# A hybrid attention block on one core: separate scrap tiles and ScalarE-issued first loads in the output projection, and the plain pair of the down projection moved to the end of its second half

## The chip, the cores and the metric

The kernel runs on one core of a Trainium2 chip. The metric is device time in microseconds of one execution. Before the change three executions took 3287.35, 3281.6 and 3287.61 us (median 3287.35).

## What is computed

One trunk layer on x of 2048 tokens by 1024 channels, in float32. `u` is the normalised input; a combined input projection feeds forgetting attention (8 heads) and an RWKV-7 scan (8 heads), whose outputs stand side by side. What the change touches comes after that:

```python
mix = concatenate([o_fox, o_rwkv], axis=-1) @ w_out      # 2048x1024 @ 1024x1024
h = h + rmsnorm(mix, attn_norm_post)
z = rmsnorm(h, ffn_norm_pre)
f = (silu(z @ w_gate) * (z @ w_up)) @ w_down             # 1024 -> 2816 -> 1024
h = h + rmsnorm(f, ffn_norm_post)
```

## The kernel before

All products run as three fp32r matmuls (`mm3`, lines 76 to 80): each operand is split into a high part (a ScalarE cast) and a low part (a subtraction on VectorE or GpSimd), and high x high, high x low and low x high are summed in PSUM. The kernel is written with a tile framework: a tile pool hands out buffers by tag, an instruction that needs a buffer waits for the last reader of what was in it, and a scheduler orders each engine's instructions by program order and by when it thinks them ready; each engine and each DMA queue then runs strictly in that order. The stages follow each other in time as: input projection, attention with the scan woven in (to about 1611 us), mix, gate and up (from about 1911 us), down (from about 2796 us).

**The mix** (class `Mix`, lines 1010 to 1169). `project` walks the 16 token tiles of 128 in pairs, in the order `m.tiles` (2 to 7, 0, 1, 8 to 15; line 1020). For each pair and each half d of the 1024 output columns it makes one product of 24 matmuls per tile into a PSUM bank of pool `e_q` (6 banks), 32 products in all; ScalarE then squares the bank into a scrap tile `njunk` for the row sums (line 1119) and copies it to `na` (line 1120; 3 buffers). `fetch` (1069) loads a tile's attention output in two halves `er` from DRAM on the SP queue, and `load` (1076) splits them into `emh` and `eml`. The first half of the first tile in this order is fetched at the end of `phase_b` (line 1205), the others in `project`. `others` loads and splits the second half of the output weights.

`norm` (1133) follows a tile: it loads x into `nx` (2 buffers), makes the factor, scales `na` on VectorE (1144), adds x on GpSimd (1145), squares again on ScalarE into `njunk` (1147), stores h, scales (1152, ScalarE), transposes eight blocks on TensorE (1158), scales into `nz` on VectorE (1160) and stores z by the SP queue (1161). The scrap tiles and the z tiles have the same tag:

```python
junk = m.pn.tile([128, 512], BF16, tag="nz", name="njunk")    # lines 1118 and 1146
zs = m.pn.tile([128, 4, 128], F32, tag="nz", name="nz")       # line 1159
```

Pool `e_n` has two buffers for that tag. `weave` (line 1722) interleaves projecting, norms and the start of the FFN (`Ffn.start`: first weights, and from the moment that eight tiles are normed the loads and splits of z for the first half, lines 1297 to 1337). `ffn.open` then makes the FFN's pools in the space that the mix's weights and tiles leave, and `quad` begins its products (`gp`).

**The down projection** (lines 1478 to 1695). The 2048 tokens are two halves of 1024, each of two blocks of 512 tokens (`b`), each of four tiles (`tt`). The 2816 hidden channels are 11 pairs of 256. Ten pairs go in five chunks of two through a seven-product scheme (Winograd's form of Strassen's) over two token blocks and two column blocks: `down_prep` makes the operands `dop` (casts at 1538, subtractions at 1540, differences at 1550), `multiply` forms the products 1, 7, 6, 5, 2, 3, 4 (line 1681), each for four tiles in 6 matmuls a tile, and `put` adds them to accumulators `acc` (the first time a ScalarE copy, line 1642; then VectorE, 1645). The 11th pair is multiplied plainly, four products of four tiles, into the accumulators 2 to 5. In both halves this happens in the first chunk (n == 0, lines 1568 to 1578 and 1685 to 1695). In the last chunk `result` (1657) combines the accumulators (1661 to 1669): a2 and a3 are the columns of token block 0, a4 and a5 those of block 1; `finish` (1613) squares them (ScalarE, 1619), makes the factor (1620, 1621, 69 to 73), multiplies by factor and gain in one instruction (1625) and adds the residual `fht` (1626: GpSimd, and VectorE for the last block of the second half), then stores. The accumulators have one buffer each, so the second half's first write of an accumulator waits for the first half's last reader.

Of the kernel before, what the change touches and what calls it, by code (L numbers as in the profile page):

```python
# [10 lines left out]
F32 = mybir.dt.float32  # L11
# [998 lines left out]
class Mix:  # L1010


    def __init__(m, k, tc, ctx, ins, scr):
        m.k, m.nc, m.ins, m.scr = k, tc.nc, ins, scr
# [54 lines left out]
    def fetch(m, tt):  # L1069
        t = slice(tt * 128, (tt + 1) * 128)  # L1070
        for i in range(2):
            r = m.r([128, 4, 128])
            m.nc.sync.dma_start(out=r, in_=m.scr["mixT"][i * 512:(i + 1) * 512, t].rearrange("(j p) t -> p j t", p=128))
            m.raws[tt, i] = r
# [14 lines left out]
    def project(m, ready):  # L1089
# [3 lines left out]
        ops = {tt: m.load(tt) for tt in m.tiles[0:2]}  # L1093
        others = m.others()
        for p in range(0, n, 2):
# [4 lines left out]
            for d in range(2):  # L1100
                for e, tt in enumerate(pair):
# [16 lines left out]
                    junk = m.pn.tile([128, 512], BF16, tag="nz", name="njunk")  # L1118
# [14 lines left out]
    def norm(m, tt, a, s2):  # L1133
# [8 lines left out]
        for d in range(2):  # L1142
# [3 lines left out]
            junk = m.pn.tile([128, 512], BF16, tag="nz", name="njunk")  # L1146
# [61 lines left out]
class Ffn:  # L1208
# [304 lines left out]
    def down_prep(f):  # L1513
# [41 lines left out]
        for i, (half, n, pairs) in enumerate(seq):  # L1555
# [12 lines left out]
            if n == 0:  # L1568
# [13 lines left out]
            if n > 0 and i + 1 < len(seq):  # L1582
                which = 1 - which
                nxt = load(i + 1)
# [7 lines left out]
            raw = nxt  # L1592

    def down(f):
# [3 lines left out]
        with ExitStack() as ctx:  # L1598
# [14 lines left out]
            def finish(t0, parts, ht, last):  # L1613
                sq = p1.tile([128, 512], F32, tag="fsq", name="fsq")
                s2 = p1.tile([128, 2], F32, tag="fs2", name="fs2", bufs=4)
                ss = p1.tile([128, 1], F32, tag="fss", name="fss", bufs=4)
                rs = p1.tile([128, 1], F32, tag="frs", name="frs", bufs=4)
                for d, a in enumerate(parts):
                    nc.scalar.activation(sq, a, AF.Square, accum_out=s2[:, d:d + 1])
# [3 lines left out]
                for d, a in enumerate(parts):  # L1623
                    c = slice(d * 512, (d + 1) * 512)
                    V.scalar_tensor_tensor(a, a, rs, gp[:, c], op0=ALU.mult, op1=ALU.mult)  # L1625
                    (V if last else G).tensor_tensor(ht[:, c], ht[:, c], a, op=ALU.add)
# [9 lines left out]
            for half in range(f.NHALF):  # L1636
                acc, hts = {}, {}
# [18 lines left out]

                def result(i, tt):
# [9 lines left out]
                    elif i in (3, 4):  # L1667
                        b, parts = (0, (a2, a3)) if i == 3 else (1, (a4, a5))
                        V.tensor_tensor(parts[4 - i], parts[4 - i], a6 if i == 3 else a7, op=ALU.add)  # L1669
                        t0 = half * f.TH + b * f.TQ + tt * 128  # L1670
                        ht = hts.get((tt, b)) or residual(p1.tile([128, D], F32, tag="fht", name="fht", bufs=4), t0)
                        finish(t0, parts, ht, half == f.NHALF - 1 and b == 1)

                for n in range(last + 1):
                    if n == last and half == f.NHALF - 1:
                        for tt in range(NT):
# [80 lines left out]
```

## Time and profile before

| | us |
|---|---|
| median of three executions | 3287.35 |
| the profiled execution, time | 3288.36 |
| its span, first to last instruction | 3286.7 |
| TensorE (PE) busy | 3015.9 |
| VectorE (DVE) busy | 2279.5 |
| ScalarE (ACT) busy | 1573.7 |
| GpSimd (POOL) busy | 1408.8 |

Busy time is summed over the span; matmul ends are modelled, so a full PE is not PE at its peak. Rows of waits name the waiting instruction, then what it waited for. In rows of a timeline a bracket at the end is the time that the engine stood idle ahead of the instruction, and what released it. SPq is the DMA queue that SyncE issues, POOLq that of GpSimd. The granted clock is a share of 2.4 GHz; 0.5 is the lower level of 1.2 GHz.

### The profile page before, as it was taken

How to read it: one execution, taken by the hardware profiler on the slowest of the kernel's cores; microseconds unless marked ns; L12 is line 12 of the kernel's file. 1: busy time of each engine (PE TensorE's matmuls, PEld its weight loads, DVE VectorE, ACT ScalarE, POOL GpSimd, SP SyncE). 2: the span in 40 equal slices, each digit the busy share in tenths (PEclk: the TensorE clock that was granted, in tenths of full speed). 3: DMA queues.
4: the chain of work that ended last, by engine and by line, in shares of the span. 5: the costliest groups of instructions: out<-in, count | busy, mean ns of one | idle time of the engine just before them, and what ended most of it. 6: DMA issues, size and time to landing. Idle time of an engine off the chain costs nothing. (4 is left out here: it accounts for less than half of the span.)

```text
span 3286.7 us, 48864 instructions
## 1 busy us (share of the span) xinstructions
PE 3015.9 (92%) x16913; PEld 2508.6 (76%) x16913; DVE 2279.5 (69%) x4846; ACT 1573.7 (48%) x3325; POOL 1408.8 (43%) x1098
## 2 busy tenths in 40 slices
PE   7999999999899999999797589999999999998895
PEld 5777777777788889888685477788788887786684
DVE  6876687665577777777545455655866556589898
ACT  5444444433677777777543332333433333544442
POOL 3444454444111111111233367433543334788886
PEclk9999999999999999999898789999999999999997
DMA  4756666667434334332345356322322223442552
GB/s 130 193 146 174 188 161 163 161 174 203 145 109 119 103 102 118 102 118 66 99 132 169 115 180 220 113 77 89 104 93 88 90 77 133 165 151 96 188 171 77
DMA packets 466877, 435.67 MB, mean 133 GB/s; under 512 B 137684, under 2 KB 383494, under 8 KB 464582
## 3 DMA queue, kind: packets, MB, share of 16 engines
q1 hardware_dynamic: 440118, 400.48, 39.8%
q0 software_dynamic: 6912, 19.93, 2.0%
q10 hardware_dynamic: 19600, 12.13, 1.4%
q8 instruction: 135, 2.21, 0.3%
q14 instruction: 112, 0.92, 0.1%
HBM read 303.59 MB, written 128.84 MB: 132 GB/s over the span
## 5 line engine op out<-in xcount | busy, mean ns | idle before, releaser
L255 POOL TENSOR_TENSOR wl<-wraw,wh 128x1024 fp32r<-128x1024 f32 (+1 forms) x108 | 268.8, 2492 | 289.7 <-ACT wh L254 287.5
L1266 ACT CAST wh<-fraw 128x512 fp32r<-128x512 f32 x308 | 186.1, 618 | 412.3 <-PE gp L79 205.7
L1270 POOL TENSOR_TENSOR wl<-fraw,wh 128x512 fp32r<-128x512 f32 x132 | 184.5, 1398 | 420.0 <-ACT wh L1266 415.4
L78 PE MATMUL mm<-uh,wh 128*128 128x512 f32 (+1 forms) x864 | 348.4, 404 | 1.1 <-DVE ol L527 1.1
L80 PE MATMUL mm<-uh,wl 128*128 128x512 f32 (+1 forms) x864 | 345.3, 400 | 0.0
L79 PE MATMUL mm<-ul,wh 128*128 128x512 f32 (+1 forms) x864 | 344.8, 399 | 0.0
L78 PE MATMUL gp<-dop 128*128 128x512 f32 x624 | 244.9, 398 | 33.3 <-ACT acc L1642 25.9
L79 PE MATMUL gp<-dop 128*128 128x512 f32 x624 | 245.6, 395 | 1.7 <-POOL dop L1540 1.7
L80 PE MATMUL gp<-dop 128*128 128x512 f32 x624 | 244.1, 395 | 0.0
L976 POOL TENSOR_TENSOR ot<-ot,rb 64x256 f32<-64x256 f32 x64 | 46.3, 723 | 426.1 <-ACT rb L975 426.1
L1540 POOL TENSOR_TENSOR dop<-dcol,dop 128x512 fp32r<-128x512 f32 x140 | 215.2, 1553 | 28.2 <-ACT dop L1538 20.4
L78 PE MATMUL gp<-za,wh 128*128 128x512 f32 x528 | 210.1, 398 | 6.6 <-ACT na L1120 5.0
L1270 DVE TENSOR_TENSOR wl<-fraw,wh 128x512 fp32r<-128x512 f32 x176 | 155.4, 883 | 84.8 <-ACT wh L1266 80.9
L955 DVE TENSOR_TENSOR tl<-pt,th 128x512 fp32r<-128x512 f32 (+1 forms) x280 | 162.8, 592 | 71.3 <-ACT th L953 68.1
L79 PE MATMUL gp<-za,wh 128*128 128x512 f32 x528 | 209.6, 397 | 0.0
L80 PE MATMUL gp<-za,wl 128*128 128x512 f32 x528 | 209.5, 397 | 0.0
L909 DVE CUSTOM_DVE_ANT_0 P<-S,ng 128x512 f32<-128x512 f32 (+2 forms) x320 | 183.8, 605 | 28.3 <-PE pt L947 15.4
L1538 ACT CAST dop<-draw 128x512 fp32r<-128x512 f32 x160 | 97.7, 620 | 220.3 <-PE gp L80 89.1
L78 PEld LDWEIGHTS mm<-uh,wh 128*128 128x128 f32 (+1 forms) x864 | 165.0, 191 | 43.1 <-issue 3.5
L1645 DVE TENSOR_TENSOR acc<-gp,acc 128x512 f32<-128x512 f32 x256 | 167.3, 680 | 42.5 <-PE gp L80 42.2
L80 PEld LDWEIGHTS mm<-uh,wl 128*128 128x128 f32 (+1 forms) x864 | 165.4, 191 | 37.4 <-issue 0.2
L920 ACT ACTIVATE P<-P,nmx 128x896 f32<-128x896 f32 (+7 forms) x248 | 187.5, 761 | 13.3 <-DVE nmx L914 12.7
(382 smaller groups left out, 8568.8 us busy)
## 6 DMA issues: line engine op xcount, KB each, us to landing
wraw<-in_w_in SPq DMA_DIRECT2D x104, 512.0 KB
fraw<-in_ffn_w_gate SPq DMA_DIRECT2D x22, 1024.0 KB
fraw<-in_ffn_w_up SPq DMA_DIRECT2D x22, 1024.0 KB
scr_hid<-s SPq DMA_DIRECT2D x22, 1024.0 KB
draw<-scr_hid SPq DMA_DIRECT2D x22, 1024.0 KB
scr_a<-A SPq DMA_DIRECT2D x16, 1280.0 KB
A<-scr_a SPq DMA_DIRECT2D x64, 320.0 KB
dcol<-scr_wt SPq DMA_DIRECT2D x40, 512.0 KB
```

What stands on the lines that cost most here:

```text
L78: nc.tensor.matmul(out, lhsT=wh, rhs=xh, start=first, stop=False)
L79: nc.tensor.matmul(out, lhsT=wh, rhs=xl, start=False, stop=False)
L80: nc.tensor.matmul(out, lhsT=wl, rhs=xh, start=False, stop=last)
L255: nc.gpsimd.tensor_tensor(wl[:, :, 0:m], raw[:, :, 0:m], wh[:, :, 0:m], op=ALU.subtract)
L909: nc.vector.tensor_tensor_reduce(out=P[:, c0:c0 + n], in0=S[:, 0:n], in1=ng[c0 // 512][:, 0:n], op0=ALU.add, op1=ALU.max, scale=1.0, scala ...
L920: nc.scalar.activation(P[:, x0:x1], P[:, x0:x1], AF.Exp, bias=nmx, accum_out=ls[:, qi, i:i + 1])
L955: nc.vector.tensor_tensor(tl[:, w[0], w[1]], pt[:, w[0], w[1]], th[:, w[0], w[1]], op=ALU.subtract)
L1266: f.nc.scalar.copy(h, x)
L1270: e.tensor_tensor(l[:, c], x[:, c], h[:, c], op=ALU.subtract)
L1538: f.nc.scalar.copy(r[0][p][i], x)
L1540: e.tensor_tensor(r[1][p][i], x, r[0][p][i], op=ALU.subtract)
L1645: V.tensor_tensor(a, ps, a, op=ALU.add)
```

## The change

It has three parts.

1. In the mix the squares' scrap has a tag of its own, `nj` (two buffers of 1 KB a partition).
2. The attention outputs of the first two tiles in the order are loaded by the ScalarE queue, and their loads and splits in `project` are made at high priority of the scheduler.
3. In the second down half the plain pair is no longer multiplied in the first chunk but behind the last one, as four products `direct` into the accumulators that `result` has completed, without the difference that the seven-product form needed; its hidden activations and weights are loaded as a sixth chunk would be, and the residuals go to the slots that the last chunk's loads leave and to `fht`. In both halves the epilogue is written anew: the gain is multiplied in by an instruction of its own (GpSimd for the first column half, VectorE for the second) beside the square, and the last scaling adds the residual in the same VectorE instruction, in place.

```diff
--- before.py
+++ after.py
@@ -1011,7 +1011,7 @@
 
 
     def __init__(m, k, tc, ctx, ins, scr):
-        m.k, m.nc, m.ins, m.scr = k, tc.nc, ins, scr
+        m.k, m.tc, m.nc, m.ins, m.scr = k, tc, tc.nc, ins, scr
         m.pw = [ctx.enter_context(tc.tile_pool(name="e_w", bufs=1, side="right"))]
         m.pr = ctx.enter_context(tc.tile_pool(name="e_r", bufs=1, side="right"))
         m.w = [[None] * NJ, [None] * NJ]
@@ -1070,7 +1070,7 @@
         t = slice(tt * 128, (tt + 1) * 128)
         for i in range(2):
             r = m.r([128, 4, 128])
-            m.nc.sync.dma_start(out=r, in_=m.scr["mixT"][i * 512:(i + 1) * 512, t].rearrange("(j p) t -> p j t", p=128))
+            (m.nc.scalar if tt in m.tiles[0:2] else m.nc.sync).dma_start(out=r, in_=m.scr["mixT"][i * 512:(i + 1) * 512, t].rearrange("(j p) t -> p j t", p=128))
             m.raws[tt, i] = r
 
     def load(m, tt):
@@ -1090,7 +1090,8 @@
 
         nc = m.nc
         n = m.k.T // 128
-        ops = {tt: m.load(tt) for tt in m.tiles[0:2]}
+        with m.tc.high_priority():
+            ops = {tt: m.load(tt) for tt in m.tiles[0:2]}
         others = m.others()
         for p in range(0, n, 2):
             a = {}
@@ -1115,7 +1116,7 @@
                     if d == e and p + 2 + d < n:
                         ops[m.tiles[p + 2 + d]] = m.load(m.tiles[p + 2 + d])
                     c = slice(d * 512, (d + 1) * 512)
-                    junk = m.pn.tile([128, 512], BF16, tag="nz", name="njunk")
+                    junk = m.pn.tile([128, 512], BF16, tag="nj", name="njunk")
                     nc.scalar.activation(junk, ps, AF.Square, accum_out=a[tt][1][:, d:d + 1])
                     nc.scalar.copy(a[tt][0][:, c], ps)
                     if d == 1:
@@ -1143,7 +1144,7 @@
             c = slice(d * 512, (d + 1) * 512)
             nc.vector.scalar_tensor_tensor(a[:, c], a[:, c], rs, m.g[:, c], op0=ALU.mult, op1=ALU.mult)
             nc.gpsimd.tensor_tensor(x[:, c], a[:, c], x[:, c], op=ALU.add)
-            junk = m.pn.tile([128, 512], BF16, tag="nz", name="njunk")
+            junk = m.pn.tile([128, 512], BF16, tag="nj", name="njunk")
             nc.scalar.activation(junk, x[:, c], AF.Square, accum_out=s2[:, d:d + 1])
             yield
         nc.gpsimd.dma_start(out=scr["h"][t, :], in_=x)
@@ -1565,7 +1566,7 @@
             add(s2, a22, s3, ALU.subtract)
             with_column(s2)
             yield
-            if n == 0:
+            if n == 0 and half < f.NHALF - 1:
                 which = 1 - which
                 h, w = f.down_load(f.hslots[which], (hid[half], f.NP - 1), (f.ins["ffn_w_down"][0], f.NP - 1))
                 for t in range(2):
@@ -1579,9 +1580,9 @@
             add(s1, a21, a22, ALU.add)
             with_column(s1)
             yield
-            if n > 0 and i + 1 < len(seq):
+            if nxt is None:
                 which = 1 - which
-                nxt = load(i + 1)
+                nxt = load(i + 1) if i + 1 < len(seq) else f.down_load(f.hslots[which], (hid[half], f.NP - 1), (f.ins["ffn_w_down"][0], f.NP - 1))
             with_column(a12)
             yield
             add(s4, a12, s2, ALU.subtract)
@@ -1590,6 +1591,11 @@
             with_column(a22)
             yield
             raw = nxt
+        h, w = raw
+        f.spare = f.hslots[1 - which]
+        for t in range(2):
+            ops([h[:, j, t] for j in range(2)], [w[:, j, t] for j in range(2)])
+            yield
 
     def down(f):
         nc, tc, scr, out = f.nc, f.tc, f.scr, f.out
@@ -1610,20 +1616,22 @@
                 nc.scalar.dma_start(out=ht, in_=scr["h"][t0:t0 + 128, :])
                 return ht
 
-            def finish(t0, parts, ht, last):
+            def square(a, s2, d, e):
+
                 sq = p1.tile([128, 512], F32, tag="fsq", name="fsq")
-                s2 = p1.tile([128, 2], F32, tag="fs2", name="fs2", bufs=4)
+                nc.scalar.activation(sq, a, AF.Square, accum_out=s2[:, d:d + 1])
+                e.tensor_tensor(a, a, gp[:, d * 512:(d + 1) * 512], op=ALU.mult)
+
+            def finish(t0, s2, parts, ht):
+
                 ss = p1.tile([128, 1], F32, tag="fss", name="fss", bufs=4)
                 rs = p1.tile([128, 1], F32, tag="frs", name="frs", bufs=4)
-                for d, a in enumerate(parts):
-                    nc.scalar.activation(sq, a, AF.Square, accum_out=s2[:, d:d + 1])
                 V.tensor_tensor(ss, s2[:, 0:1], s2[:, 1:2], op=ALU.add)
                 V.tensor_scalar(ss, ss, 1.0 / D, NORM_EPS, op0=ALU.mult, op1=ALU.add)
                 rsqrt2(nc, p4, rs, ss, "frq")
                 for d, a in enumerate(parts):
                     c = slice(d * 512, (d + 1) * 512)
-                    V.scalar_tensor_tensor(a, a, rs, gp[:, c], op0=ALU.mult, op1=ALU.mult)
-                    (V if last else G).tensor_tensor(ht[:, c], ht[:, c], a, op=ALU.add)
+                    V.scalar_tensor_tensor(ht[:, c], a, rs, ht[:, c], op0=ALU.mult, op1=ALU.add)
                 nc.sync.dma_start(out=out[t0:t0 + 128, :], in_=ht)
 
             def product(terms):
@@ -1634,7 +1642,8 @@
 
             last = len(f.chunks()) - 1
             for half in range(f.NHALF):
-                acc, hts = {}, {}
+                acc, hts, s2s = {}, {}, {}
+                plain_last = half == f.NHALF - 1
 
                 def put(i, tt, ps):
                     if (i, tt) not in acc:
@@ -1653,6 +1662,24 @@
                             put(i, tt, ps)
                             if n == last:
                                 result(i, tt)
+
+                def direct(x, y, i, b, d):
+
+                    for tt in range(NT):
+                        t = slice(tt * 128, (tt + 1) * 128)
+                        ps = product([(x[0][p][0][:, t], x[1][p][0][:, t], y[0][p][1], y[1][p][1]) for p in range(2)])
+                        put(i, tt, ps)
+                        ready(b, tt, d)
+
+                def ready(b, tt, d):
+                    i = 2 + 2 * b + d
+                    if d == 0:
+                        s2s[b, tt] = p1.tile([128, 2], F32, tag="fs2", name="fs2", bufs=8)
+                    square(acc[i, tt], s2s[b, tt], d, G if d == 0 else V)
+                    if d == 1:
+                        t0 = half * f.TH + b * f.TQ + tt * 128
+                        ht = hts.get((tt, b)) or residual(p1.tile([128, D], F32, tag="fht", name="fht", bufs=4), t0)
+                        finish(t0, s2s[b, tt], (acc[i - 1, tt], acc[i, tt]), ht)
 
                 def result(i, tt):
 
@@ -1665,24 +1692,21 @@
                     elif i == 2:
                         G.tensor_tensor(a2, a2, a1, op=ALU.add)
                     elif i in (3, 4):
-                        b, parts = (0, (a2, a3)) if i == 3 else (1, (a4, a5))
-                        V.tensor_tensor(parts[4 - i], parts[4 - i], a6 if i == 3 else a7, op=ALU.add)
-                        t0 = half * f.TH + b * f.TQ + tt * 128
-                        ht = hts.get((tt, b)) or residual(p1.tile([128, D], F32, tag="fht", name="fht", bufs=4), t0)
-                        finish(t0, parts, ht, half == f.NHALF - 1 and b == 1)
+                        V.tensor_tensor(acc[i, tt], acc[i, tt], a6 if i == 3 else a7, op=ALU.add)
+                        if not plain_last:
+                            if i == 3:
+                                ready(0, tt, 0)
+                                ready(0, tt, 1)
+                            else:
+                                ready(1, tt, 0)
+                                ready(1, tt, 1)
 
                 for n in range(last + 1):
-                    if n == last and half == f.NHALF - 1:
-                        for tt in range(NT):
-                            pool, tag = f.hslots[1 - half % 2 if tt < 2 else half % 2][tt % 2]
-                            r = pool.tile([128, 2, D], F32, tag=tag, name="fht")
-                            for i in range(2):
-                                hts[tt, i] = residual(r[:, i], half * f.TH + i * f.TQ + tt * 128)
                     for i in (1, 7, 6, 5, 2, 3, 4):
                         x = f.dops.pop(0)
                         multiply(x, x, i)
                         next(f.dp, None)
-                        if n == 0 and i == 6:
+                        if n == 0 and i == 6 and not plain_last:
                             x = f.dops.pop(0)
                             multiply(x, x, 2)
                             next(f.dp, None)
@@ -1693,6 +1717,21 @@
                             x = f.dops.pop(0)
                             multiply(x, y, 3)
                             next(f.dp, None)
+                if plain_last:
+                    x = f.dops.pop(0)
+                    next(f.dp, None)
+                    y = f.dops.pop(0)
+                    for tt in range(NT):
+                        if tt % 2 == 0:
+                            pool, tag = f.spare[tt // 2]
+                            r = pool.tile([128, 2, D], F32, tag=tag, name="fht")
+                        hts[tt, 1] = residual(r[:, tt % 2], half * f.TH + f.TQ + tt * 128)
+                    for tt in range(NT):
+                        hts[tt, 0] = residual(p1.tile([128, D], F32, tag="fht", name="fht", bufs=4), half * f.TH + tt * 128)
+                    direct(x, x, 2, 0, 0)
+                    direct(x, y, 3, 0, 1)
+                    direct(y, x, 4, 1, 0)
+                    direct(y, y, 5, 1, 1)
 
 
 @with_exitstack
```

## Rows read from the trace of the kernel before

**Rows 1.** Head of the page.

```profile
span 3286.7 us, 48864 instructions
```

**Rows 2.** Windows: us, then PE, PEld, DVE, ACT, POOL busy (instructions), PEclk, DMA.

```profile
1611.00:1626.50 15.50, 0.00 (x0) 0.00 (x0) 6.35 (x4) 5.68 (x11) 8.90 (x7) 0.60 1.02 326
1626.50:1731.40 104.90, 104.86 (x472) 86.50 (x472) 36.92 (x99) 40.06 (x93) 35.74 (x28) 0.98 0.45 143
1731.40:1852.00 120.60, 95.12 (x393) 75.67 (x392) 59.18 (x123) 50.00 (x111) 41.70 (x29) 0.87 0.43 143
1852.00:1911.00 59.00, 15.23 (x58) 12.11 (x57) 33.43 (x72) 25.00 (x53) 22.61 (x16) 0.59 0.29 100
```

**Rows 3.** Waits of PE, 1600 to 1735: us in total, times, longest.

```profile
PE eps L78 <- ACT emh L1085: 16.7, 1, 16.7
PE eps L78 <- ACT na L1120: 1.4, 1, 1.4
```

**Rows 4.** Waits of PE, 1735 to 1915.

```profile
PE npt L1158 <- ACT na L1152: 41.1, 5, 22.5
PE eps L78 <- ACT na L1120: 21.8, 8, 7.1
```

**Rows 5.** Waits of ACT, 1735 to 1915.

```profile
ACT njunk L1119 <- DMA scr_z<-nz: 40.0, 7, 8.9
ACT njunk L1147 <- POOL nx L1145: 21.1, 8, 8.2
...
ACT njunk L1147 <- DMA scr_z<-nz: 4.3, 1, 4.3
```

**Rows 6.** Timeline of ACT: start, us, instruction, idle before.

```profile
1765.13 0.60 ACT L1119 ACTIVATE njunk<-eps 128x512 bf16<-128x512 f32 x1 [8.90 <-DMA scr_z<-nz]
```

**Rows 7.** Waits of ACT, 1640 to 1735.

```profile
ACT njunk L1119 <- DMA scr_z<-nz: 35.5, 5, 9.2
```

**Rows 8.** Windows of the down halves, columns as in rows 2.

```profile
3002.00:3074.00 72.00, 47.93 (x166) 35.47 (x166) 65.39 (x93) 35.00 (x85) 59.93 (x41) 0.86 0.40 145
3074.00:3200.00 126.00, 125.97 (x556) 103.95 (x555) 110.49 (x140) 56.45 (x104) 108.88 (x73) 1.00 0.50 168
...
3248.20:3286.70 38.50, 0.00 (x0) 0.00 (x0) 34.84 (x85) 10.33 (x34) 13.36 (x9) 0.55 0.27 109
```

**Rows 9.** Timeline, one tile's norm early in the mix and one late.

```profile
1647.34 0.82 DVE L1128 TENSOR_TENSOR nss<-ns 128x1 f32<-128x1 f32 x1 [0.36 <-ACT njunk L1119]
...
1649.91 1.42 DVE L1144 SCALAR_TENSOR_TENSOR na<-na,nrs,eg 128x512 f32<-128x512 f32 x2
...
1867.03 1.41 DVE L1144 SCALAR_TENSOR_TENSOR na<-na,nrs,eg 128x512 f32<-128x512 f32 x2
...
1874.51 0.90 PE L1158 MATMUL npt<-ident,na 128*128 128x128 f32 x3 [22.49 <-ACT na L1152]
```

**Rows 10.** First load; DMA issues (KB each, us to landing) of 1608:1616 and of all.

```profile
1614.81 2.94 SPq L1073 DMA_DIRECT2D er<-scr_mixT  x1
...
1625.87 0.62 ACT L1085 CAST emh<-er 128x512 fp32r<-128x512 f32 x1 [3.02 <-DMA er<-scr_mixT]
...
scr_mixT<-ot POOLq DMA_DIRECT2D x2, 64.0 KB, 5.3
...
scr_mixT<-ot POOLq DMA_DIRECT2D x64, 64.0 KB, 2.2
```

**Rows 11.** Groups by line, 3002 to 3074: busy, mean ns; idle before, releaser.

```profile
L78 PE MATMUL gp<-dop 128*128 128x512 f32 x56 | 24.5, 470 | 22.3 <-ACT acc L1642 15.0 <-DVE acc L1645 7.2
...
L1625 DVE SCALAR_TENSOR_TENSOR acc<-acc,frs,fgp 128x512 f32<-128x512 f32 x16 | 18.3, 1190 | 0.0
...
L1550 DVE TENSOR_TENSOR draw<-draw 128x512 f32<-128x512 f32 x7 | 8.3, 1195 | 0.0
```

**Rows 12.** Groups by line, 3248 to 3287.

```profile
L1626 DVE TENSOR_TENSOR fht<-fht,acc 128x512 f32<-128x512 f32 x8 | 5.1, 679 | 0.0
```

**Rows 13.** Timeline of PE, its last wait between the halves.

```profile
3063.97 0.80 PE L78 MATMUL gp<-dop 128*128 128x512 f32 x1 [7.16 <-ACT acc L1642]
```

## The prediction

> **What bounds the kernel now.** I read the page first, then the waits of the engine that is busiest, then the same stretches by windows. One profiled execution spans 3286.7 us [rows 1] inside a time of 3288.36 us, 1.0 us above the median of the three runs (3287.35); the sum below is made against 3288.4. TensorE is nearly always busy; the change touches three places where it isn't: the mix (1611 to 1911 us), the change from one down half to the next (3002 to 3074) and the end.
>
> The mix, in four stretches [rows 2]: 15.5 us without a matmul; 104.9 us full; 120.6 us in which TensorE is busy for 95 at a granted clock of 0.87; 59 us with 15.2 us of work at 0.59 (1 is the level of 2.4 GHz, 0.5 that of 1.2). The first gap is one wait of 16.7 us for ScalarE's cast of the first tile [rows 3]. The full stretch holds 18 of the 32 products (x432 of the 768 matmuls) and five tiles' transposes, so a product with its share of transposes takes 104.9 / 18 = 5.83 us. The 14 others would take 81.6 us at that pace and took 120.6: 39.0 us lost, of which 21.8 are waits for the copy out of PSUM (line 1120) and 2.3 of the 41.1 us a wait of transposes [rows 4]; the other 14.9 are the lower clock that follows each wait. The last stretch waits for the norms of the last four tiles.
>
> Why is ScalarE late? It works only 50 us of the 120.6 [rows 2], but its queue is in order, and the squares of lines 1119 and 1147 wait for the store of z, 40.0 and 4.3 us here [rows 5], because scrap and z tiles share the two buffers of tag "nz". One example [rows 6]: ScalarE stands still for 8.9 us ahead of a square at 1765.13 although its product is long done. From 1640 to 1735 the same wait costs ScalarE 35.5 us [rows 7] and TensorE 1.4 [rows 3]: six PSUM banks absorb it until ScalarE has fallen behind by six products. So it is a debt that grows and is paid after 1731.
>
> The down half: between 3002 and 3074 VectorE is busy 65 of 72 us and TensorE 48; at the end TensorE stops at 3248.2 and VectorE works 34.8 of the last 38.5 us [rows 8].
>
> **Part 1, own buffers.** Nothing is added but 2 KB of tiles. All writers of "nj" are ScalarE itself, so its reuse waits for nobody; z tiles now wait for a store one tile back, which is long landed. What is late next is the norm's own chain: ScalarE still waits 21.1 us for GpSimd's additions [rows 5], and the loads and splits of the FFN's z share VectorE and GpSimd. Before the last product ends I credit the 24.1 us of plain waits and leave the 14.9 us of clock, since those other waits will go on making short gaps: **24 us**, bounds 0 and 39.
>
> After the last product (1852 to 1911) TensorE waits for tiles that are two to three behind; the thirteenth tile's norm scales only at 1867.03 [rows 9], 15 us after the very last product. With no debt, the last tile's squares follow its product at once. From a square to the first scaling takes 2.6 us (1647.34 to 1649.91), from there to the transposes 7.5 us (1867.03 to 1874.51) [rows 9], so 59 us could become about 12, in which the 24 FFN matmuls done there now still fit: 47 us at most. But VectorE has 33.4 us of work in that stretch [rows 2], mostly FFN splits that begin when the mix weights are released. I take 29 us as what remains, a little under VectorE's work since two tiles' norms have moved ahead of it: **30 us**, bounds 0 and 47. The FFN that follows is bound by TensorE, so the shift reaches the end.
>
> **Part 2, first loads from ScalarE's queue, at high priority.** Four loads of 256 KB leave SP's queue. There the first is issued at 1614.81, right behind the other half of the output weights and the first FFN weights, and its cast starts at 1625.87, 11 us later; in the same stretch two 64 KB stores on GpSimd's queue landed in 5.3 us against 2.2 over the whole run [rows 10]. A queue of its own therefore shares with the backlog instead of standing behind it. I take 5.5 us to landing instead of 11 (the nearest row, of a smaller transfer in the same traffic): **5.5 us**. Bounds: 0, if it lands as late as now, and 8.8 at 2.2 us. It can't be issued earlier, as it reads one of those stores. ScalarE's queue holds the trigger meanwhile; behind it stand only casts of weights that land later. One of the four is issued during the attention already; a wait there on ScalarE costs at most the 2.2 us that such a store takes to land, which PSUM banks may absorb, so I set nothing.
> The Trainium skill, page "DMA: Bandwidth & Descriptors", section "Issuing engines are not separate DMA queues", says that transfers of all issuing engines interleave on the same 16 DMA engines and that spreading them saves only the sequencer's time. By that rule this part gives nothing and the forecast would be 5.5 us later; the two stores that landed in half of the load's time do not agree with it.
>
> **Part 3, the plain pair at the end.** Of the second half 16 products of 6 matmuls move from its first chunk behind its last; at 126.0 us / 556 matmuls [rows 8] they are 21.8 us. Gone are one difference (2 VectorE additions, 1.2 us each), 2 casts and 2 subtractions [rows 11]. New are 8 multiplications by the gain on VectorE and 8 on GpSimd per half; gone are 16 additions to the residual, because the last scaling now adds.
>
> At the change of halves VectorE gets 8 x 1.2 = 9.5 us more and loses 2.4 for the difference and some 3.6 for three subtractions, taken at the same 1.2 [rows 11]: 3.5 us more. GpSimd loses 16 additions for 8 multiplications, and 7 subtractions; VectorE's operations are longer beside GpSimd's (1.19 us there, 0.68 for one of like size in the tail [rows 11, 12]). I set the sum to 1 us. TensorE has less to do meanwhile: today its last wait there ends at 3063.97 [rows 13], and the matmuls left until 3248.2, 6 to a product, are those of 134 of the half's 156 products, so 22 are done by then. In the new order there are 20 to do until a5 comes free: products 1, 7 and 6 (12) and eight in PSUM banks. Two products, 2.7 us, are lost. So the chunks end at 3248.2 - 21.8 + 2.7 + 1 = 3230.1.
>
> From there VectorE has its present 34.8 us, less 8 residual additions (5.4), plus 16 additions out of PSUM (10.9) and 8 multiplications (5.4), all at 0.68 [rows 8, 12]: 45.7, of which 21.8 lie under TensorE's last products. With the 3.7 us that follow VectorE's work now (38.5 less 34.8, the last store) it ends at 3279.5: **7 us** gained. Bounds: -11, if TensorE loses all 21.8 us at the change of halves (3248.2 + 45.7 + 3.7), and +18 if VectorE's backlog there vanishes with GpSimd's work.
>
> **Sum**: 24 + 30 + 5.5 + 7 = 66.5; 3288.4 - 66.5 = 3221.9, against the median **3221**.
>
> **Rivals.**
> - *The norm chain keeps the pace.* The store was only the last of several waits; squares now wait for GpSimd's additions and for VectorE under the FFN splits. For it: 21.1 us of such waits today [rows 5]; against: in the full stretch ScalarE works 40 of 105 us [rows 2]. Half of part 1: 27 + 5.5 + 7 = 39.5, so 3248. Chance 0.20.
> - *The loads gain nothing*, being in the same traffic: 3227. The two stores at 5.3 us speak against it. Chance 0.08. This is the Trainium skill's rule of part 2.
> - *All debt goes*, TensorE runs through the mix: 39 + 47 + 8.8 + 7, so 3186. It needs the FFN splits to hide wholly. Chance 0.04.
> - *The change does not do it*: the squares wait as long for another buffer, as the x tiles (also two). Only parts 2 and 3: 3275 to 3287. The x loads were never what GpSimd waited for. Chance 0.07.
> - *Slower*: the change of halves. Accumulators a5 and a4 are freed last by the first half's norm, and the second half now needs a5 as its fourth product instead of its sixth, with no plain products to fill; TensorE stands for the whole 21.8 us and the end comes 10.9 us later than now: with nothing from part 1 and 2, 3298. It decides only if these give under 11 us. TensorE waits 22.3 us there now [rows 11], which speaks for a real wait; the eight PSUM banks against. Chance 0.06.
>
> **Numbers.** The forecast has 0.55, with 3203 to 3242 as its own range. 3200 to 3262 takes in most of the first rival and leaves out the extremes, about 2 in 10. A measurement can tell 0.2%, 6.6 us, from no change. Faster: 0.55 + 0.20 + 0.08 + 0.04 + over half of the fourth = 0.91; same 0.03; slower 0.06.
>
> **What would show it.** Right: no wait of lines 1119 or 1147 for the store of z; the last mix product near 1815 to 1830 instead of 1852; FFN matmuls without a break within 30 us of it; the first product near 1621; TensorE stopping within 5 us of 3248 less the shift, and VectorE 30 us later at most. Wrong: squares or copies that wait as long for line 1145 or 1144, transposes that wait over 10 us, or over 40 us of waits at the change of halves.

## The result and the profile after

The changed kernel takes 3216.97 us (median of four executions, 3213.96 to 3220.16) against 3287.48 beside it: ratio 0.9781, 95% interval 0.9765 to 0.9797. The forecast was 3221. The profiled execution took 3220.16 us. The stretches in which its span and that of the kernel before differ (us):

| stretch | before | after | less | forecast |
|---|---|---|---|---|
| start to the first mix product | 1626.5 | 1627.1 | -0.5 | 5.5 |
| first to last mix product | 225.5 | 195.6 | 29.9 | 24 |
| from there to unbroken FFN products | 58.9 | 30.0 | 28.9 | 30 |
| gate and up, first down half | 1091.1 | 1088.9 | 2.2 | 0 |
| change of halves to the end | 284.7 | 276.8 | 7.9 | 7 |
| span | 3286.7 | 3218.3 | 68.4 | 66.5 |

The fourth stretch took 1088 to 1093 us in the profiles of the kernels below, so its 2.2 us are no finding. The windows of the changed kernel, columns as in [rows 2]: the mix in four stretches, the change of halves, the direct products, and what follows TensorE's last product.

```profile
1611.70:1627.06 15.36, 0.00 (x0) 0.00 (x0) 6.37 (x5) 5.90 (x12) 8.88 (x7) 0.61 1.01 325
1627.06:1732.00 104.94, 104.94 (x477) 87.15 (x478) 45.10 (x129) 52.60 (x125) 42.36 (x34) 0.98 0.54 171
1732.00:1822.60 90.60, 87.25 (x406) 72.68 (x405) 61.31 (x129) 47.92 (x107) 41.99 (x29) 0.96 0.58 185
1822.60:1852.60 30.00, 10.48 (x42) 7.38 (x40) 26.65 (x38) 14.77 (x25) 20.23 (x11) 0.68 0.36 122
2941.50:3014.00 72.50, 48.47 (x153) 35.01 (x154) 72.30 (x102) 40.18 (x94) 57.26 (x37) 0.81 0.40 139
3168.70:3198.60 29.90, 24.48 (x97) 18.83 (x95) 27.73 (x52) 9.78 (x30) 22.98 (x16) 0.94 0.00 1
3198.60:3218.30 19.70, 0.02 (x1) 0.00 (x0) 15.97 (x52) 2.82 (x10) 0.00 (x0) 0.59 0.53 213
```

Beside [rows 2] the first stretch is as long as it was, the second is the same, the third has lost 30 us and its granted clock has gone from 0.87 to 0.96, the fourth is half as long with VectorE busy for nearly all of it. The last row is the old 38.5 us of [rows 8].

Waits of TensorE (PE) in the changed kernel, 1735 to 1860, then of ScalarE (ACT) in the same stretch:

```profile
PE npt L1159 <- ACT na L1153: 17.7, 3, 9.7
PE gp L79 <- POOL zb L1271: 2.8, 1, 2.8
PE gp L79 <- DVE zb L1271: 2.2, 1, 2.2
```

```profile
ACT nrs L70 <- DVE nq L69: 20.1, 9, 7.6
ACT njunk L1148 <- POOL nx L1146: 16.9, 13, 3.4
```

The 21.8 us of TensorE's waits for a copy out of PSUM [rows 4] are gone, and no square waits for a store of z any more [rows 5, 7]. What ScalarE waits for now is VectorE and GpSimd in the norm's own chain.

The first load, in the changed kernel's timeline:

```profile
1615.69 0.95 ACTq L1073 DMA_DIRECT2D er<-scr_mixT  x2
...
1626.39 1.89 ACT L1085 CAST emh<-er 128x512 fp32r<-128x512 f32 x3 [3.13 <-DMA er<-scr_mixT]
1627.06 0.79 PE L78 MATMUL eps<-ewh,emh 128*128 128x512 f32 x1 [16.37 <-ACT emh L1085]
```

It leaves on ScalarE's queue, and is cast 10.7 us after its issue; on SP it was 11.1 [rows 10].

### The profile page after: what moved, and what is told of

The parts are those of the page before. It is cut to its first block, busy times and chain, and to the rows that moved or that the text cites. A ratio compares the mean times of both kernels' runs of the same rounds, so it can differ in the third digit from the quotient of the medians.

```text
span 3218.3 us, 48871 instructions
## 1 busy us (share of the span) xinstructions
PE 3008.4 (93%) x16913; PEld 2506.8 (78%) x16913; DVE 2283.0 (71%) x4852; ACT 1574.7 (49%) x3323; POOL 1393.6 (43%) x1088
## 5 line engine op out<-in xcount | busy, mean ns | idle before, releaser
L255 POOL TENSOR_TENSOR wl<-wraw,wh 128x1024 fp32r<-128x1024 f32 (+1 forms) x108 | 261.8, 2427 | 291.6 <-ACT wh L254 290.1
L78 PE MATMUL gp<-dop 128*128 128x512 f32 x624 | 249.6, 402 | 36.7 <-ACT acc L1651 18.6
L79 PE MATMUL gp<-dop 128*128 128x512 f32 x624 | 247.9, 399 | 3.1 <-POOL dop L1541 3.1
L80 PE MATMUL gp<-dop 128*128 128x512 f32 x624 | 247.0, 399 | 0.0
L79 PEld LDWEIGHTS mm<-ul,wh 128*128 128x128 f32 (+1 forms) x864 | 165.2, 191 | 37.3 <-issue 1.7
```

The lines of the kernel that those rows point to most:

```text
L78: nc.tensor.matmul(out, lhsT=wh, rhs=xh, start=first, stop=False)
L79: nc.tensor.matmul(out, lhsT=wh, rhs=xl, start=False, stop=False)
L80: nc.tensor.matmul(out, lhsT=wl, rhs=xh, start=False, stop=last)
L255: nc.gpsimd.tensor_tensor(wl[:, :, 0:m], raw[:, :, 0:m], wh[:, :, 0:m], op=ALU.subtract)
```

## Experiments

All ratios are to the kernel before, run beside. In the profiles the attention's last store lies between 1609 and 1618 us, so stretches are compared, not moments: "load to cast" is from the issue of the first tile's last mix load to its cast, "to product" from the attention's last store to the first mix product, "mix" from there to unbroken FFN products, "down" from TensorE's first wait at the change of halves to the end.

| kernel | ratio | 95% interval | load to cast | to product | mix | down |
|---|---|---|---|---|---|---|
| before | 1 | | 11.1 | 14.2 | 284.4 | 284.7 |
| changed | 0.9781 | 0.9765 to 0.9797 | 10.7 | 13.9 | 225.5 | 276.8 |
| own scrap alone | 0.9818 | 0.9802 to 0.9835 | 11.0 | 14.2 | 224.8 | 284.6 |
| early loads alone | 1.0004 | 0.9992 to 1.0016 | 10.9 | 14.2 | 286.4 | 284.9 |
| down part alone | 0.9977 | 0.9968 to 0.9987 | 11.2 | 14.4 | 284.1 | 276.8 |
| changed, no early loads | 0.9792 | 0.9776 to 0.9809 | 10.1 | 13.6 | 224.8 | 275.2 |
| weights behind (misplaced) | 0.9791 | 0.977 to 0.9812 | 11.4 | 14.7 | 226.0 | 276.8 |
| new epilogue alone | 0.9995 | 0.9981 to 1.001 | 11.0 | 14.3 | 287.0 | 283.9 |
| plain pair last alone | 1.0009 | 0.9997 to 1.002 | 10.0 | 14.1 | 284.9 | 286.1 |
| three shared buffers | 0.9914 | 0.9889 to 0.9939 | 10.6 | 14.2 | 248.0 | 285.0 |
| block first | 0.9763 | 0.9748 to 0.9778 | 4.7 | 5.5 | 224.3 | 276.8 |
| one block by ScalarE | 0.9785 | 0.9765 to 0.9805 | 9.2 | 12.4 | 227.5 | 276.8 |
| half the backlog | 0.9789 | 0.9767 to 0.9811 | 7.3 | 11.1 | 225.3 | 276.7 |
| new epilogue in the second half | 0.9988 | 0.9978 to 0.9998 | 10.6 | 14.0 | 284.7 | 283.0 |

### Own scrap alone

```
-junk = m.pn.tile([128, 512], BF16, tag="nz", name="njunk")   # lines 1118 and 1146
+junk = m.pn.tile([128, 512], BF16, tag="nj", name="njunk")
```

> Edit: the kernel before with one thing changed, the squares' scrap in two buffers of its own (tag nj). Theory (the coupling of ScalarE's squares to the stores of z was the whole of the mix's loss): ratio 0.982, some 3229 us, 58 us less; the mix's product takes 196 us instead of 225, the tail after its last product 30 us instead of 59, and no square waits for a store. Rival A (the order of work that the early first loads bring is needed too): only the tail or only the product shrinks, 24 to 35 us less, ratio 0.989 to 0.993. Rival B (the norm chain hits another buffer): under 15 us less.

Measured 3229.77 us. Its windows, product and tail:

```profile
1626.20:1819.10 192.90, 189.52 (x881) 157.26 (x882) 104.94 (x253) 100.17 (x230) 84.75 (x62) 0.99 0.57 179
1819.10:1851.00 31.90, 12.34 (x42) 8.63 (x40) 28.29 (x42) 15.32 (x27) 20.21 (x11) 0.60 0.35 119
```

Both shrink as in the changed kernel: two tags in two lines are the whole gain of the mix.

### Early loads alone

```
+with m.tc.high_priority():
+    ops = {tt: m.load(tt) for tt in m.tiles[0:2]}
 in fetch: (m.nc.scalar if tt in m.tiles[0:2] else m.nc.sync).dma_start(...)
```

> Edit: the kernel before with only the first mix loads issued by ScalarE and traced at high priority. Theory (a queue of its own shares the DMA engines with the weights' backlog, so the block lands as late as before): within 3 us of the kernel before, ratio 0.999 to 1.001, first mix product at 1626 to 1628 us. Rival A (prediction's term, 5.5 us, that other work hid in the changed kernel): ratio 0.998, first product at about 1621. Rival B (the early priority reorders the norms and loosens the scrap's coupling by itself): 10 us less or more, ratio under 0.997.

No gain: the ratio is 1.0004, give or take 0.0012. Its timeline has the load on ScalarE's queue and the cast 10.9 us later:

```profile
1617.15 0.94 ACTq L1073 DMA_DIRECT2D er<-scr_mixT  x2
...
1628.10 1.14 ACT L1085 CAST emh<-er 128x512 fp32r<-128x512 f32 x2 [2.68 <-DMA er<-scr_mixT]
```

The moment of the first product missed the band named (1628.8), as the attention ended later; measured from its last store it is 14.2 us, as before.

### The changed kernel without the early loads

The changed kernel without the edit of the section before this one.

> Edit: the changed kernel with its first mix loads back on SP's queue and at their old priority; the scrap's own buffers and the plain pair at the end stay. Theory (the early loads are worth nothing): same as the changed kernel within 3 us, 3217, ratio 0.978 to 0.9795, first mix product at about 1627. Rival A (the loads' priority keeps the norms ahead and is worth the part of the mix that the scrap alone does not give): 3225 or more, ratio over 0.981. Rival B (issuing them from ScalarE costs ScalarE): 3213 or less.

Measured 3220.69 us, the same as the changed kernel within the intervals, which are too wide to exclude 5.5 us by themselves. The profiles say more: the first product comes 13.6 us after the last store without the early loads and 13.9 with them, so there was no gain there for other work to hide.

### Down part alone

Only the changes in the last two functions of the diff, `down_prep` and `down`.

> Edit: the kernel before with only the down part of the change (the plain pair last in the second half, squares and gain ahead of the factor). Theory: 8 us less, ratio 0.9976, about 3279.5; TensorE stops about 20 us before the end instead of 39, and its last product is later than before by about 11 us. Rival A (the down part is worth more, and part of the mix's gain was lost between the two): 12 us or more less, ratio under 0.9965. Rival B (it is worth nothing without the earlier start that the mix gives): within 2 us of the kernel before.

Measured 7.4 us less by the medians. Its windows of the change of halves and of the end:

```profile
3004.40:3076.00 71.60, 47.69 (x151) 34.56 (x151) 71.39 (x101) 40.12 (x93) 56.95 (x38) 0.81 0.40 136
3261.50:3281.20 19.70, 0.04 (x1) 0.00 (x0) 15.96 (x52) 2.83 (x10) 0.00 (x0) 0.59 0.53 213
```

The end is that of the changed kernel to two hundredths of a us; the part needs nothing from the mix. Counted from the change of halves TensorE stops 11 us later than before, and the 38.5 us behind it are 19.7.

### New epilogue alone, plain pair last alone, and between them

The first keeps the plain pair in the first chunk; the second keeps the old epilogue:

```
-e.tensor_tensor(a, a, gp[:, d * 512:(d + 1) * 512], op=ALU.mult)
-V.scalar_tensor_tensor(ht[:, c], a, rs, ht[:, c], op0=ALU.mult, op1=ALU.add)
+V.scalar_tensor_tensor(a, a, rs, gp[:, c], op0=ALU.mult, op1=ALU.mult)
+(V if last else G).tensor_tensor(ht[:, c], ht[:, c], a, op=ALU.add)
```

> Edit: the kernel before with only the new epilogue in both halves (gain multiplied ahead of the factor, one fused operation for scaling and residual); the plain pair stays in the first chunk. Theory (the down part's 8 us come from what VectorE still has to do after the last product): the closing stretch without products shrinks from 38.5 us by some 3 us, one VectorE operation of 0.7 us less for each of four tiles; ratio 0.9985 to 0.9995. Rival A (the epilogue is all of it): ratio 0.9977 or less. Rival B (GpSimd's multiplications hold VectorE up at the change of halves): slower, ratio over 1.001.

> Edit: the kernel before with only the plain pair moved to the end of the second half, with the old epilogue (squares, scaling by gain and factor, separate residual addition). Theory: most of the 8 us, since the plain products at the end run beside the additions and norms of earlier tiles; 4 to 7 us less, ratio 0.998 to 0.9988, closing stretch without products 20 to 26 us. Rival A (the move without the shorter epilogue brings nothing, as GpSimd's residual additions close the kernel): within 2 us. Rival B (the move is all of it): 8 us or more less, ratio 0.9976 or less.

Neither half of the down part is worth anything by itself, against the theory on the second; and the theory on the first had the closing stretch 3 us shorter, where it is as long as before. The end of the first; then, of the second, its end and TensorE's largest wait at the change of halves (3000 to 3110):

```profile
3255.20:3293.70 38.50, 0.00 (x0) 0.00 (x0) 34.72 (x85) 10.46 (x34) 14.07 (x9) 0.56 0.27 109
```

```profile
3265.20:3289.50 24.30, 0.00 (x0) 0.00 (x0) 20.69 (x54) 5.79 (x19) 6.93 (x5) 0.56 0.38 151
```

```profile
PE gp L78 <- ACT acc L1648: 20.5, 4, 8.6
```

With the epilogue alone VectorE still has 34.7 us to do at the end: it is moving the pair that shortens the end. With the move alone the end is 14.2 us shorter, but TensorE waits 29.2 us at the change of halves instead of 23.9 (22.3 of it in [rows 11], the rest for GpSimd), since the plain products that used to fill it are gone, and stops 15.6 us later. In the down part alone these waits are 23.7 us. So in the moved order the new epilogue takes 5.5 us off the waits at the change of halves and 4.6 off the end; in the old order it has next to nothing to shorten. The same kernel with the new epilogue in the second half only:

> Edit: the kernel with the down part alone, but its new epilogue only in the second half; the first half keeps the old one (square, gain and factor together, GpSimd's residual addition). Theory (the epilogue pays in two places: it takes 5 us of TensorE's idle time at the change of halves, where the first half's epilogue runs, and 5 us of the closing stretch): from the end of the first half's steady products to the end of the kernel about 281.5 us, against 276.8 with the new epilogue in both halves, 286.1 with the old one in both and 284.7 before; closing stretch 19.7 us; ratio to the kernel before 0.9985 to 0.9995. Rival A (only the end counts): 277 to 278 us, ratio 0.9977. Rival B (only the change of halves counts): 285 to 286 us, closing stretch 24 us, ratio 1.000 or more.

```profile
3268.00:3287.60 19.60, 0.00 (x0) 0.00 (x0) 15.91 (x52) 2.83 (x10) 0.00 (x0) 0.61 0.53 214
```

```profile
PE gp L78 <- ACT acc L1655: 19.5, 4, 8.7
```

The end is 19.6 us again and the waits at the change of halves stay at 29.9: both places count, 283.0 us for 281.5 expected.

### Three shared buffers

```
-tag="nz", name="njunk"            and   tag="nz", name="nz"
+tag="nz", name="njunk", bufs=3    and   tag="nz", name="nz", bufs=3
```

> Edit: the kernel before with scrap and stored z still in one rotation, but of three buffers instead of two: about the memory that the change spends on scrap of its own. Theory (it is the sharing: a square that follows a stored tile in the rotation still waits for that store, only one place later): a part of the gain, 15 to 45 us less, ratio 0.986 to 0.9955, and squares still wait for stores. Rival A (any further buffer does it): 58 us less, ratio 0.982, no such wait left. Rival B (one buffer more does not matter): under 10 us less.

28 us less, in the theory's range, but not by its reason. Windows of product and tail, and the waits of ScalarE for a store, 1735 to 1915:

```profile
1629.10:1825.50 196.40, 189.64 (x864) 156.33 (x864) 95.09 (x224) 90.84 (x206) 78.68 (x57) 0.98 0.49 157
1825.50:1877.10 51.60, 14.07 (x58) 11.60 (x57) 35.82 (x71) 24.47 (x50) 25.58 (x16) 0.59 0.44 143
```

```profile
ACT njunk L1147 <- POOL nx L1145: 26.5, 13, 4.7
...
ACT njunk L1147 <- DMA scr_z<-nz: 2.9, 1, 2.9
...
ACT njunk L1119 <- DMA scr_z<-nz: 1.0, 1, 1.0
```

One buffer more takes nearly all waits for stores away, and the product stretch is nearly as short as with own scrap (196.4 us, 192.9). The tail is not: five of ScalarE's copies of mix products come after the last product (six before, one with own scrap), and its squares wait for GpSimd. Whether that is the order in which the queues were written or the norm's chain running late wasn't separated. Nor was a rotation of four shared buffers run, as many tiles as own scrap has in its two tags, so how much of the gain is the separation and how much the number of buffers stays open.

### What holds the first load: the weights ahead of it

> Edit: the changed kernel with its first mix loads back on SP, and the second half of w_out, the norm's gain and the first gate weights (3.5 MB) issued on SP behind the first tile's last load instead of ahead of it. Theory (the backlog on the DMA engines, and not the queue that carries the loads, sets their landing): from the load's issue to its first cast 3 to 6 us instead of 10.1 to 11.2, the first mix product 5 to 7 us earlier after the last store of the attention, and 4 to 7 us less in the whole against the same kernel with the old order of the weights: about 3213, ratio 0.977. Rival A (the landing is set by something else, such as the size of the transfer's pieces): first cast no earlier than 9 us after the issue, time as it was. Rival B (the weights are then late): the first product is earlier, but a product with the second half of w_out waits for its weights and the gain is under 2 us.

This run did not do what its text says. `fetch` at line 1205 asks for both blocks of the first tile: one leaves early in the attention, at 1068 us, and the one that the first product waits for at 1616.68. The edge stood on the early one, and SP's queue kept its order, as its timeline shows; it repeats the kernel without early loads and its time:

```profile
1612.32 1.89 SPq L1061 DMA_DIRECT2D ewr<-in_w_out  x3
1616.68 8.15 SPq L1075 DMA_DIRECT2D er<-scr_mixT  x4
```

Mended, and with half of it:

```
+m.sent.append(m.last)                       # in fetch; all mix loads on SP
+with m.tc.issue_after(m.sent[0]):           # around ewr, eg and the first gate weights
+    nc.sync.dma_start(...)                  # half the backlog: around eg and the gate weights
```

> Edit: as the weights-behind kernel, but the second half of w_out, the norm's gain and the first gate weights stand on SP behind the load that the first product waits for (the block of mixT that the attention writes last); the edge stood on the other block of that tile there, which leaves early in the attention, so that nothing moved. Theory (backlog on the DMA engines sets the landing): from this load's issue to its cast 3 to 5 us instead of 10.1 to 11.2, the first mix product 6 to 8 us earlier after the attention's last store, and 4 to 8 us less than the changed kernel if no product then waits for the weights: ratio 0.9755 to 0.977. Rival A (the landing is set by the transfer's small pieces, not by what is ahead): cast no earlier than 9 us after the issue. Rival B (the weights, now late, are waited for): the first product is earlier, but a later product waits for the second half of w_out, and under 2 us remain.

> Edit: as the block-first kernel, but only the norm's gain and the first gate weights (1.5 of the 3.5 MB) stand behind the first tile's last load; the second half of w_out stays ahead of it. Theory (the landing is when what is ahead has drained): between the two, cast 4.5 to 7 us after the issue, some 4 us or more earlier than in the changed kernel, first product 4 to 6 us earlier, 3 to 6 us less in the whole, ratio 0.9762 to 0.9772. Rival A (the landing hangs on something else): cast 10 us after the issue, no gain. Rival B (any transfer ahead holds it as long): cast within 1 us of the changed kernel's although 1.5 MB less stand ahead.

Block first, timeline:

```profile
1616.48 0.59 POOL L977 DMA_DIRECT2D scr_mixT<-ot  x1 [0.30 <-POOL ot L976]
1616.63 0.92 SPq L1075 DMA_DIRECT2D er<-scr_mixT  x2
...
1621.31 1.14 ACT L1088 CAST emh<-er 128x512 fp32r<-128x512 f32 x2 [5.93 <-DMA er<-scr_mixT]
...
1621.98 0.80 PE L78 MATMUL eps<-ewh,emh 128*128 128x512 f32 x1 [8.02 <-ACT emh L1088]
```

With no weights ahead the same load is cast 4.7 us after its issue, and the first product comes 5.5 us after the last store instead of 13.9. Of these 8.4 us, 6.0 are the load's; the others come before it is issued, since the store that it waits for, on GpSimd's queue, now lands 2.7 us after its issue instead of 5.0. No later product of the mix waits for weights. From the last store to the end of the span it is 1598.1 us against 1605.1 in the changed kernel: 7.0 us less. The median, 3213.45 us, is the lowest of all, and the ratio 0.0018 (5.9 us) below the changed kernel's, but the two intervals overlap, so the runs don't settle the size of this gain. That there is one is likely: all five executions (3210.12 to 3216.52) lie below all five of the changed kernel without early loads (3217.11 to 3225.51), with the kernel before at 3289.06 and 3290.05 beside them.

With half the backlog the cast came 7.3 us after the issue, late for the 4.5 to 7 us of the theory, but it stood by then behind ScalarE's casts of the weights:

```profile
1623.39 4.25 ACT L1041 CAST ewh<-ewr 128x512 fp32r<-128x512 f32 x8 [6.87 <-issue]
1627.55 1.13 ACT L1087 CAST emh<-er 128x512 fp32r<-128x512 f32 x2
```

The packets of 512 bytes on SP's queue, which are those of the mix loads, ran from 1623.2 to 1626.0, so the load had landed within about 6 us of its issue. The first product came 2.8 us earlier than in the changed kernel where 4 to 6 were expected, and the time shows no gain (ratio 0.9789, expected 0.9762 to 0.9772). So the run agrees with the theory on the landing and missed on what it is worth.

```
-(m.nc.scalar if tt in m.tiles[0:2] else m.nc.sync)
+(m.nc.scalar if tt == m.tiles[0] else m.nc.sync)
```

> Edit: the changed kernel with only the first tile's mix loads issued by ScalarE; the second tile's are back on SP. Theory (the two queues alternate packet by packet, and the two blocks on ScalarE's queue share its half): the first block lands some 2 to 3 us earlier, cast 7.5 to 9 us after the issue instead of 10.7, first product 2 to 3 us earlier; time as the changed kernel or 2 to 3 us less. Rival A (a queue of its own makes no difference at any size): cast again 10 to 11 us after the issue. Rival B (without the second block nothing is left in the way): cast under 6 us after the issue.

The view of the DMA queues (packets, MB, share of 16 engines; q1 is SP's queue, q10 ScalarE's) of the changed kernel, for 1618 to 1620 and 1622 to 1624:

```profile
q1 hardware_dynamic: 357, 0.74, 104.4%
q10 hardware_dynamic: 14, 0.01, 1.2%
...
q1 hardware_dynamic: 439, 0.45, 71.3%
q10 hardware_dynamic: 441, 0.22, 41.5%
```

and with one block on ScalarE's queue, issued at 1611.65, for 1614 to 1616, 1616 to 1618 and 1618 to 1620:

```profile
q10 hardware_dynamic: 6, 0.00, 0.5%
...
q1 hardware_dynamic: 263, 0.61, 80.4%
q10 hardware_dynamic: 208, 0.11, 18.1%
...
q10 hardware_dynamic: 300, 0.15, 26.7%
```

In both, nothing of ScalarE's queue moves until some 4 us after the issue (first packet between 1619.5 and 1620, and between 1615.5 and 1616), and once it is under way it gets about one packet of two (441 beside 439; with one block 208 beside 263, its start included). A block is 512 packets of 512 bytes; the two, issued together, were through by 1626, one alone was nearly through at 1620. In the block-first kernel, with the engines idle, SP's first packets moved between 1617.5 and 1618, some 1 us after the issue at 1616.63; its queue from 1616 to 1618:

```profile
q1 hardware_dynamic: 45, 0.02, 4.0%
```

That is SP's queue. ScalarE's own is no slower to start: in the changed kernel the other block of the first tile, issued on it at 1065.96 with the engines at a share of 0.57, moved its first packets 1.1 us later. Its queue from 1067 to 1068 (from 1066 to 1067 it has none):

```profile
q10 hardware_dynamic: 484, 0.24, 84.7%
```

The one block by ScalarE was cast 9.2 us after its issue, 1.5 earlier than with two (2 to 3 were expected), and then the second tile's block, back behind the weights, made TensorE wait 2.2 us more. The time is that of the changed kernel.

## Why the prediction held, step by step

That the sum came within 2 us (68.4 for 66.5) is in part luck: the 6.0 us that part 2 fell short by were made up by 5.9 more than was credited in the mix.

**Part 1, right.** The store's waits were the debt, and removing them alone gives the mix's gain (own scrap alone). Until the last product 24 us were credited and 29.9 came: the term left the 14.9 us of lowered clock where they were, but the clock rose with the waits' end (0.87 to 0.96), and of the 39.0 us lost against the full stretch's pace about 9 are left (90.6 less 81.6). The tail kept 30.0 us for 29 foreseen, with VectorE busy 26.7 of them, as the bound by VectorE's work had it. The first rival, the norm chain keeping the pace, took only what had been left for it.

**Part 2, wrong: 5.5 us forecast, none came.** The first product was to come near 1621 and came at 1627.1. The step that failed is "a queue of its own therefore shares with the backlog instead of standing behind it", with the landing of a 64 KB store taken for that of a 256 KB block. It does share, but too little: 4 us pass before its first packet, 3 more than on idle engines, and then it moves one packet for each of SP's, which carried twice the bytes (0.22 MB to 0.45), while two blocks split its half. What decides is the 3.5 MB of weights put on the engines just ahead (block first). The rival given 0.08 was this one, and should have had more. The Trainium skill, page "DMA: Bandwidth & Descriptors", section "Issuing engines are not separate DMA queues", says that issuing transfers on several engines saves only issue time; the 10.7 us here beside 11.1 agree. Its section "Queues, rings and completion order" has the DMA engines go round the queues by packets, and the 441 packets beside 439 agree.

**Part 3, right in sum, by a finer balance than was argued.** The chunks were to end at 3230.1 before the shift of the stretches above, the kernel 49.4 us later (45.7 and 3.7); the direct products began near 3168.7 and the end came 49.6 us after. Counted from the change of halves, the chunks end after 227.2 us, where 228.1 were forecast. One sign was missed: TensorE, set at 21.8 us for the direct products, takes 29.9, 24.5 of them busy, and stops 11 us later than the 3248 less the shift, not within 5. The end shows none of it, since VectorE closes the kernel as argued, with 43.7 us of work (27.7 and 16.0) for 45.7 and 5.9 us idle for 3.7. At the change of halves 3.5 us more for VectorE were set against GpSimd's relief and netted to 1 us, with two products lost. The runs show the two sums: the move costs 5.3 us of TensorE's waits there, and the epilogue gives 5.5 back. What is lost there all the same, 2.8 us to the chunks' end (227.2 less 224.4, which is the 246.2 of before without the plain pair's 21.8) for 3.7 forecast, isn't in the waits: the granted clock is 0.81 there instead of 0.86 [rows 8], and the profile has 153 matmuls in 72.5 us where it had 166 in 72.0. The slower rival is the first of these at a quarter of its price.

## What to carry to other kernels

When a scratch tile shares a rotation with a tile that is being stored, the engine that writes the scratch can come to wait for a DMA it has nothing to do with; look for an in-order engine that is half idle while others wait for it, and give the scratch a tag of its own. A late load that stood in heavy traffic wasn't helped here by another queue; what helped it was to hold the large transfers that weren't yet needed behind it. Of a change in several parts, measure each alone and all but each: two parts that are worth nothing singly were worth 8 us together here.

## What the runs showed of the hardware

In this traffic a transfer on an otherwise empty queue, issued while SP's queue kept the engines at a share near 1, began to move only some 4 us later (from 1615.69 to 1619.5 at least; with one block from 1611.65 to 1615.5 at least); on idle engines it was 1 us. The share alone doesn't set this delay: in the changed kernel two other transfers on ScalarE's queue, issued at 781.13 and 3001.42 with the engines at shares of 0.96 to 1.07 in the 2 us on either side, moved their first packets 1.2 and 3.1 us later. What sets it was not found. Between 1622 and 1624 the two queues moved equal numbers of packets, 441 and 439, whatever their size, so the one with pieces of 512 bytes got a third of the bytes.
